# Seven-product steps of passes 6 and 7 of the MLP placed one channel-major step later

## The chip, the core and the metric

The kernel runs on one core of one Trainium2 chip. The metric is the device time of one launch in microseconds (us), median of several runs. A profile is one execution of its own; its times are given from the start of its span.

## What is computed

A trunk of two layers on 256 tokens with 2048 channels, in fp32. Each layer is

```
h = rms_norm(x, norm1_g[l]);  z = h @ w_in[l]            # attention heads and gMLP groups from z
x = x + mix @ w_out[l]                                   # mix: both kinds of groups side by side
h2 = rms_norm(x, norm2_g[l])
x = x + jnp.square(jax.nn.relu(h2 @ w_up[l])) @ w_down[l]   # 2048 -> 8192 -> 2048
```

and a last rms_norm follows. The change lies in the last line, the MLP, of both layers.

## The kernel before, in words

**Products.** Each fp32 factor is split into a high part and a remainder, and a product is three matmuls: high x high, high x remainder of the weight, remainder of the activation x high. Weights come from memory in blocks of 128 x 1024 ("raw", seven buffers), issued by SyncE. ScalarE (ACT) copies a block into its high part ("hi", line 168, six buffers), VectorE (DVE) subtracts that to get the remainder ("lo", line 178, six buffers). So TensorE (PE) needs one hi and one lo for each block.

**Steps.** The program is a list of steps, run in order by the loop at lines 1004 to 1025. Ahead of a step's matmuls the loop issues the hi of blocks up to six on and the lo of blocks up to five on, and whatever small work is due; after them what has to be done with a finished result. A position in time ("soon", "later") is counted in blocks.

A channel-major step (`transposed`, lines 370 to 406) takes one block and makes 24 matmuls of 256 columns: a part of 256 output channels for all tokens. For `w_up` four such steps in a row fill one PSUM bank, for `w_down` two. While the MLP runs, these steps change between banks 0 and 1 (`of=2`). After the last step of a bank of `w_up`, `after_up` (line 779) empties it: ACT makes relu (785), square (788) and the high part of the result (645), DVE its remainder (648); in pass 7 DVE does the relu (787).

A seven-product step (`fast`, lines 408 to 446) multiplies with 512 columns of `w_down` by a scheme of seven products in place of eight. It has two halves, each with two raw blocks, from which DVE makes two more by four subtractions (lines 219 to 224), each gated by ACT's hi. A half takes four lo: top (line 191), bottom, upper and lower (178), in the order in which PE needs them, and counts as four blocks. It makes 42 matmuls; the last three are held back until two matmuls of the next channel-major step have been issued (`BEHIND`, `BETWEEN`).

**Banks of a seven-product step.** Group 0 (output columns 0 to 511) accumulates in held banks ("aux"). Groups 1 and 2 use banks 2 and 3 for four of their products, and borrow, for two more, that one of banks 0 and 1 which the channel-major steps don't use just then (line 863). After the second half, ACT copies the three banks to a staging buffer, the borrowed one first (lines 905 and 906), and later GpSimd's DMAs add the staging buffer to sums in DRAM (`put`, `move`). In a group's last pass (`FINAL`: pass 7 for groups 0 and 1, pass 6 for group 2) the sums are fetched instead, DVE combines them (819 to 827), ACT scales them (832), and PE turns them back by four transposes at line 844, twice.

**Passes.** The loop at line 911 goes through passes e = 0 to 8. Pass e computes hidden channels of eighth e of `w_up` (16 channel-major steps, numbers 0 to 15) and multiplies the eighth before with `w_down`: columns that are not in a group by channel-major steps that follow the up steps (four steps in passes 2 to 6, eight in 1 and 7), and the groups by seven-product steps that stand between. After up step 15, `sums` (line 798) has DVE make four sums of the finished eighth and ACT and DVE split them (645, 648); the seven-product steps of the next pass read them.

**What sets the order.** The table `ORDER` (line 63; passes not named take `USUAL`, line 66) gives for pass e and each group a pair of step numbers: the first half stands right ahead of the first, the second half right ahead of the second. Passes 2 to 5 have group 1 at (2, 3) and group 2 at (13, 14).

Of the kernel before, what the change touches and what calls it, by code (L numbers as in the profile page):

```python
# [59 lines left out]

ORDER = {1: ((7, 10), (13, 14)), 6: ((11, 14), (1, 2), (6, 7)), 7: ((6, 9), (1, 2)), 8: ()}
FINAL = (7, 7, 6)
LAST = (4, 6, 8, 10, 0, 2, 12, 14)
USUAL = ((7, 9), (2, 3), (13, 14))
# [25 lines left out]
def trunk(ctx: ExitStack, tc: tile.TileContext, layout, xT, consts, gains, w, b_sp, w_sp, out):  # L92
# [419 lines left out]
    def layer(l, n1, n2, n3, last):  # L512
# [398 lines left out]
        for e in range(9):  # L911
# [5 lines left out]
            if e:  # L917
                w = 512 * len(ORDER.get(e, USUAL))
                hidden = [hid[e - 1]]
# [3 lines left out]
                               cols=None if e < 8 else [c * P for c in LAST])  # L923
                for g, at in enumerate(ORDER.get(e, USUAL)):
                    banks = []
# [147 lines left out]
```

## Time and profile before

| | |
|---|---|
| Time, median of 3 runs (all) | 2032.55 us (2033.97, 2032.55, 2028.91) |
| The profiled execution | 2032.09 us, span 2030.3 us |
| Busy in the span | PE 99%, weight loads 98%, DVE 78%, ACT 60%, GpSimd 8% |
| Channel-major matmuls, line 404 | 5632 + 2816 on hs, 2688 + 1344 on half, 276 to 277 ns each |
| DVE remainders, line 178 | 817, 1213 ns mean |
| ACT high parts, line 168 | 817, 1051 ns mean |

A matmul lasts some 276 ns, but a new one starts every 0.113 us or so, since they are pipelined; so the share of busy time says little, and the distance between starts says how fast PE runs. In the timelines a row is a start, a duration, the engine, the line, the operation, output<-inputs, their shapes and how many of them were merged; in brackets stands how long the engine was idle ahead of it and what ended that.

### The profile page before, as it was taken

The page shows a single profiled execution, that of the slowest core. Times are in us where ns is not written, and L with a number is a line of the kernel's source. Part 1 is how long each engine was busy: PE and PEld are TensorE (multiplying, and loading weights), DVE is VectorE, ACT ScalarE, POOL GpSimd, SP SyncE. Part 2 cuts the span into 40 slices and gives each one's busy share as a digit, 9 for nine tenths or more (in the row PEclk, how much of TensorE's full clock was granted, in tenths as well). Part 3 has the DMA queues.
Part 4 walks back from the last instruction along what each step waited for, and adds up shares of the span by engine and source line. Part 5 has one row for each costly group of instructions (what it writes and reads, how often), then busy time and mean ns, then how long its engine had stood idle before and what let it go on. Part 6 is the DMA issues. An engine that isn't in the chain of part 4 may idle for free.

```text
span 2030.3 us, 40718 instructions
## 1 busy us (share of the span) xinstructions
PE 2016.9 (99%) x16834; PEld 1979.6 (98%) x16834; DVE 1576.8 (78%) x1950; ACT 1213.2 (60%) x1613; POOL 157.1 (8%) x200
## 2 busy tenths in 40 slices
PE   9999999999999999999999999999999999999997
PEld 7998999999999999999989989999999999999997
DVE  7566766688888898888856667667888898888985
ACT  7565454566566666665545654556666666667654
POOL 0002300000001000100000033000000000010000
PEclk9999999999999999999999999999999999999999
DMA  8554556567677776866664455555676776778562
GB/s 326 192 168 166 187 187 200 175 229 207 217 221 237 244 225 193 243 214 210 204 212 166 167 187 188 188 196 180 217 228 209 226 236 215 239 212 263 183 211 93
DMA packets 126443, 419.27 MB, mean 207 GB/s; under 512 B 14128, under 2 KB 22064, under 8 KB 126256
## 3 DMA queue, kind: packets, MB, share of 16 engines
q1 hardware_dynamic: 110800, 389.86, 56.6%
q0 software_dynamic: 14304, 23.86, 6.8%
q8 instruction: 132, 2.16, 0.4%
q10 hardware_dynamic: 1152, 2.94, 0.4%
q14 instruction: 55, 0.45, 0.1%
HBM read 394.58 MB, written 22.02 MB: 205 GB/s over the span
## 4 chain that ended last, share of the span: by engine, by line
PE 97%; DVE 2%; DMA 1%; ACT 0%; issue 0%; ACTq 0%; SPq 0%; DVEq 0%
PE acc L404 69%; PE acc L434 9%; PE aux L434 8%; PE acc L466 3%; PE acc L465 3%; PE acc L464 3%; DVE lo L178 1%; PE aux L698 0%; PE aux L592 0%; PE aux L634 0%; DMA raw<-in_w 0%; PE aux L621 0%; DVE x L1035 0%; DMA x<-in_xT 0%; PE aux L595 0%
## 5 line engine op out<-in xcount | busy, mean ns | idle before, releaser
L168 ACT ACTIVATE hi<-raw 128x1024 fp32r<-128x1024 f32 (+1 forms) x817 | 836.1, 1051 | 496.2 <-DVE raw L220 232.6
L178 DVE TENSOR_TENSOR lo<-raw,hi 128x1024 fp32r<-128x1024 f32 (+1 forms) x817 | 963.6, 1213 | 155.9 <-ACT hi L168 152.7
L404 PE MATMUL acc<-hs,hi 128*128 128x256 f32 x5632 | 988.1, 277 | 0.0
L404 PEld LDWEIGHTS acc<-hs,hi 128*128 128x128 f32 x5632 | 858.4, 188 | 0.3 <-issue 0.2
L404 PE MATMUL acc<-hs,lo 128*128 128x256 f32 x2816 | 779.0, 277 | 0.0
L404 PEld LDWEIGHTS acc<-hs,lo 128*128 128x128 f32 x2816 | 528.8, 188 | 0.5 <-issue 0.2
L404 PE MATMUL acc<-half,hi 128*128 128x256 f32 x2688 | 462.1, 276 | 0.0
L404 PEld LDWEIGHTS acc<-half,hi 128*128 128x128 f32 x2688 | 406.5, 188 | 0.0
L404 PE MATMUL acc<-half,lo 128*128 128x256 f32 x1344 | 371.1, 276 | 0.0
L404 PEld LDWEIGHTS acc<-half,lo 128*128 128x128 f32 x1344 | 252.4, 188 | 0.0
L871 POOL DMA_DIRECT2D far<-ar x92 | 74.7, 983 | 1158.9 <-ACT ar L874 607.0
L434 PE MATMUL acc<-hi,shared 128*128 128x256 f32 x768 | 139.1, 276 | 0.0
L434 PE MATMUL aux<-hi,half 128*128 128x256 f32 x528 | 120.6, 278 | 0.0
L434 PEld LDWEIGHTS acc<-hi,shared 128*128 128x128 f32 x768 | 119.3, 188 | 0.0
L434 PE MATMUL acc<-lo,shared 128*128 128x256 f32 x384 | 106.5, 277 | 0.6 <-DVE lo L178 0.6
L464 PE MATMUL acc<-hi,hs 128*128 128x512 f32 x256 | 101.3, 396 | 0.2 <-ACT hs L286 0.2
L466 PE MATMUL acc<-hi,hs 128*128 128x512 f32 x256 | 100.8, 394 | 0.0
L465 PE MATMUL acc<-lo,hs 128*128 128x512 f32 x256 | 100.1, 391 | 0.6 <-DVE lo L178 0.6
L648 DVE TENSOR_TENSOR half<-ar,half 128x512 fp32r<-128x512 f32 x72 | 49.7, 690 | 62.3 <-ACT half L645 61.2
L434 PEld LDWEIGHTS aux<-hi,half 128*128 128x128 f32 x528 | 92.9, 188 | 0.0
L434 PE MATMUL aux<-hi,shared 128*128 128x256 f32 x448 | 81.1, 276 | 0.0
L504 DVE TENSOR_TENSOR x<-x,acc 128x512 f32<-128x512 f32 (+1 forms) x49 | 33.0, 674 | 57.7 <-PE acc L404 57.3
(151 smaller groups left out, 1954.0 us busy)
## 6 DMA issues: line engine op xcount, KB each, us to landing
raw<-in_w SPq DMA_DIRECT2D x731, 512.0 KB, 4.6
far<-ar POOLq DMA_DIRECT2D x60, 256.0 KB, 6.3
far<-ar POOLq DMA_DIRECT2D x32, 128.0 KB, 4.4
ar<-far POOLq DMA_DIRECT2D x12, 256.0 KB, 8.9
raw<-in_w SPq DMA_DIRECT2D x10, 256.0 KB, 5.1
x<-in_xT SPq DMA_DIRECT2D x7, 256.0 KB, 5.9
out<-x SPq DMA_DIRECT2D x7, 256.0 KB, 3.0
shared<-in_b_sp ACTq DMA_DIRECT2D x2, 512.0 KB, 8.1
```

The costliest lines, as they stand in the source:

```text
L168: act.activation(self.h[:, j * m:(j + 1) * m], self.raw[:, j * m:(j + 1) * m], AF.Copy)
L178: vec.tensor_tensor(lo[:, r], self.raw[:, r], self.h[:, r].bitcast(F32), op=OP.subtract)
L404: pe.matmul(o, lhsT=lhs, rhs=xs[:, rhs, :], start=(first and j == 0), stop=(last and j == 2), skip_group_check=True)
L434: calls.append(lambda k=k, j=j, lhs=lhs, rhs=rhs: pe.matmul(o[n], lhsT=lhs, rhs=rhs, start=(p == 0 and k == 0 and j == 0 and n in fresh), ...
L464: pe.matmul(ps, lhsT=xh, rhs=hi, start=(k0 + k == 0), stop=False)
L465: pe.matmul(ps, lhsT=xh, rhs=lo, start=False, stop=False)
L466: pe.matmul(ps, lhsT=xl, rhs=hi, start=False, stop=(k0 + k == KC - 1))
L504: vec.tensor_tensor(xj, xj, ps[j][:, 0:S] if alone else pair(ps)[:, j, :], op=OP.add)
L648: vec.tensor_tensor(t[:, c:c + 2, 1, :], src, t[:, c:c + 2, 0, :].bitcast(F32), op=OP.subtract)
L871: nc.gpsimd.dma_start(far[g][:, r], src, **({} if e == max(g, 1) else {"accum_op": OP.add}))
```

## The change

The numbers of passes 6 and 7 in the table each go up by one. Every half of a seven-product step in these passes, with all that is counted from it, comes after one more channel-major step; the last entry, pass 8, has none.

```diff
-ORDER = {1: ((7, 10), (13, 14)), 6: ((11, 14), (1, 2), (6, 7)), 7: ((6, 9), (1, 2)), 8: ()}
+ORDER = {1: ((7, 10), (13, 14)), 6: ((12, 15), (2, 3), (7, 8)), 7: ((7, 10), (2, 3)), 8: ()}
```

The number of instructions stays the same on every engine, and GpSimd's order does not change. Three places show what moves, all in the first layer's pass 6.

VectorE, from the last addition of a `w_down` column of pass 5 (L772) to the lo of "upper" for the second half of group 1; L191 and the four raw rows are that half's. Before:

```order
L772 TENSOR_TENSOR ar_80<-ar_80,acc0_9460 128x512
L178 TENSOR_TENSOR lo_9523<-raw_9312,hi_9489 128x1024
L178 TENSOR_TENSOR lo_9555<-raw_9314,hi_9521 128x1024
L191 TENSOR_TENSOR lo_9603<-raw_9316,hi_9552 128x512
L178 TENSOR_TENSOR lo_9605<-raw_9318,hi_9601 128x1024
L219 TENSOR_TENSOR raw_9316<-raw_9316 128x2x256
L220 TENSOR_TENSOR raw_9316<-raw_9318,raw_9316 128x2x256
L223 TENSOR_TENSOR raw_9318<-raw_9318,raw_9316 128x2x256
L224 TENSOR_TENSOR raw_9318<-raw_9318 128x2x256
L178 TENSOR_TENSOR lo_9617<-raw_9316,hi_9609 128x1024
```

And after the change:

```order
L772 TENSOR_TENSOR ar_80<-ar_80,acc0_9458 128x512
L178 TENSOR_TENSOR lo_9523<-raw_9312,hi_9491 128x1024
L178 TENSOR_TENSOR lo_9555<-raw_9314,hi_9521 128x1024
L178 TENSOR_TENSOR lo_9585<-raw_9316,hi_9552 128x1024
L191 TENSOR_TENSOR lo_9633<-raw_9318,hi_9583 128x512
L178 TENSOR_TENSOR lo_9635<-raw_9352,hi_9631 128x1024
L219 TENSOR_TENSOR raw_9318<-raw_9318 128x2x256
L220 TENSOR_TENSOR raw_9318<-raw_9352,raw_9318 128x2x256
L223 TENSOR_TENSOR raw_9352<-raw_9352,raw_9318 128x2x256
L224 TENSOR_TENSOR raw_9352<-raw_9352 128x2x256
L178 TENSOR_TENSOR lo_9647<-raw_9318,hi_9639 128x1024
```

One lo more, that of the channel-major step that now comes earlier, stands ahead of the half's own.

TensorE, the end of the second half of group 2 and the start of the channel-major step behind it; acc0 and acc1 are banks 0 and 1, and the bank that the half has borrowed is acc1 in both. Before:

```order
L434 MATMUL acc1_9858<-hi_9910,shared_4236 128x256
L434 MATMUL aux_4476<-hi_9910,half_8722 128x256
L434 MATMUL aux_4476<-lo_9918,half_8722 128x256
L434 MATMUL aux_4476<-hi_9910,half_8722 128x256
L404 MATMUL acc0_9794<-hs_85,hi_9912 128x256
L404 MATMUL acc0_9794<-hs_85,lo_9953 128x256
```

And after the change:

```order
L434 MATMUL acc1_9888<-hi_9940,shared_4236 128x256
L434 MATMUL aux_4476<-hi_9940,half_8722 128x256
L434 MATMUL aux_4476<-lo_9948,half_8722 128x256
L434 MATMUL aux_4476<-hi_9940,half_8722 128x256
L404 MATMUL acc1_10055<-hs_85,hi_9942 128x256
L404 MATMUL acc1_10055<-hs_85,lo_9986 128x256
```

Before, the step behind is step 7, which goes on in bank 0; now it is step 8, which opens bank 1, the borrowed one.

ScalarE, from the hi of that half's "upper" to the three copies of the banks. Before:

```order
L168 ACTIVATE hi_9906<-raw_9656 128x1024
L168 ACTIVATE hi_9910<-raw_9716 128x1024
L168 ACTIVATE hi_9912<-raw_9718 128x1024
L168 ACTIVATE hi_9951<-raw_9720 128x1024
L906 ACTIVATE ar_80<-acc1_9858 128x512
L906 ACTIVATE ar_80<-acc2_9856 128x512
L906 ACTIVATE ar_80<-acc3_9857 128x512
```

And after the change:

```order
L168 ACTIVATE hi_9936<-raw_9686 128x1024
L168 ACTIVATE hi_9940<-raw_9746 128x1024
L168 ACTIVATE hi_9942<-raw_9748 128x1024
L785 ACTIVATE ar_80<-acc0_9793 128x512
L788 ACTIVATE ar_80<-ar_80 128x512
L645 ACTIVATE half_9779<-ar_80 128x2x256
L168 ACTIVATE hi_9984<-raw_9750 128x1024
L906 ACTIVATE ar_80<-acc1_9888 128x512
L906 ACTIVATE ar_80<-acc2_9886 128x512
L906 ACTIVATE ar_80<-acc3_9887 128x512
```

The relu, square and high part of up step 7's bank, which stood behind the copies, now stand ahead of them.

## The prediction

> **What bounds the kernel now.** I read the page first, then who waited for whom, then PE's timeline where it waited.
>
> ```profile
> span 2030.3 us, 40718 instructions
> PE 2016.9 (99%) x16834; PEld 1979.6 (98%) x16834; DVE 1576.8 (78%) x1950; ACT 1213.2 (60%) x1613; POOL 157.1 (8%) x200
> PE 97%; DVE 2%; DMA 1%; ACT 0%; issue 0%; ACTq 0%; SPq 0%; DVEq 0%
> PE acc L434 <- DVE lo L178: 0.6, 3, 0.2
> ```
>
> PE is the bound; the change leaves its 16834 matmuls as they are. So only PE's waits and its pace can change. The last line, from the list of waits, names the one kind of wait at line 434, a seven-product half that waits for DVE's lo: three times, 0.6 us. PE's timeline at these places, and at a fourth like them, with the matmul ahead of each wait and the two behind it:
>
> ```profile
> 807.26 0.39 PE L434 MATMUL acc<-hi,shared 128*128 128x256 f32 x2
> 807.85 0.38 PE L434 MATMUL acc<-lo,shared 128*128 128x256 f32 x1 [0.20 <-DVE lo L178]
> 808.08 0.40 PE L434 MATMUL acc<-hi,shared 128*128 128x256 f32 x2
> ...
> 894.18 0.39 PE L434 MATMUL acc<-hi,shared 128*128 128x256 f32 x2
> 894.55 0.39 PE L434 MATMUL acc<-lo,shared 128*128 128x256 f32 x1
> 894.78 0.40 PE L434 MATMUL acc<-hi,shared 128*128 128x256 f32 x2
> ...
> 1812.80 0.39 PE L434 MATMUL acc<-hi,shared 128*128 128x256 f32 x2
> 1813.39 0.39 PE L434 MATMUL acc<-lo,shared 128*128 128x256 f32 x1 [0.20 <-DVE lo L178]
> 1813.62 0.40 PE L434 MATMUL acc<-hi,shared 128*128 128x256 f32 x2
> ...
> 1897.48 0.39 PE L434 MATMUL acc<-hi,shared 128*128 128x256 f32 x2
> 1898.04 0.39 PE L434 MATMUL acc<-lo,shared 128*128 128x256 f32 x1 [0.17 <-DVE lo L178]
> 1898.27 0.28 PE L434 MATMUL acc<-hi,shared 128*128 128x256 f32 x1
> ```
>
> These are the second halves of group 1 in passes 6 and 7 of layer 0, then of layer 1, each at its first use of "upper". A row of two has its second start 0.11 behind the first, so the starts are 0.47, 0.26, 0.48 and 0.45 us apart, and then 0.23, where 0.11 is usual. A wait costs its distance less the usual 0.11, and some 0.12 in the second gap, so about the distance itself: 0.47 + 0.26 + 0.48 + 0.45 = 1.66 us.
>
> They have a consequence that no wait shows. The undisturbed pace is in a row of the chain; the stretches after it are from the table by stretches (its second column is PE's busy time, with the matmuls in brackets; the one ahead of the DMA share is the granted clock).
>
> ```profile
> 612.75 21.55 PE acc L404 x190
> 640.00:680.00 40.00, 40.00 (x355) 40.00 (x354) 35.86 (x40) 28.08 (x35) 4.38 (x5) 1.00 0.78 241
> 812.00:852.00 40.00, 40.00 (x342) 40.00 (x341) 34.84 (x39) 27.29 (x35) 6.62 (x8) 1.00 0.90 263
> 1817.00:1857.00 40.00, 40.00 (x354) 40.00 (x353) 35.41 (x40) 27.86 (x36) 6.99 (x8) 1.00 0.91 268
> 1899.00:1939.00 40.00, 40.00 (x343) 40.00 (x342) 35.00 (x42) 26.80 (x34) 4.08 (x5) 1.00 0.82 263
> 870.02 0.60 PE L844 MATMUL acc<-con,ar 128*128 128x128 f32 x4
> 876.12 0.60 PE L844 MATMUL acc<-con,ar 128*128 128x128 f32 x4
> 1936.19 0.60 PE L844 MATMUL acc<-con,ar 128*128 128x128 f32 x4
> ```
>
> Normally 21.55 / 190 = 0.1134 us a matmul. After the waits at 807 and 1898, 40 us hold 342 or 343 matmuls instead of 355, 3.7% fewer, at a clock of 1.00; after the one at 1813 they hold 354. I call this a tail. It ended at the transposes of 876 (not at those of 870) and of 1936. So two waits of four left long tails: 68.4 us x 0.037 = 2.5 us and 38.3 us x 0.037 = 1.4 us.
>
> All that these four waits cost is 1.66 + 2.5 + 1.4 = 5.6 us of 2032, 0.27%. Two runs of this kernel differ by as much (2028.91 and 2033.97), so 0.3%, some 6.1 us, is about what a measurement can tell from no change.
>
> **Part one: DVE gets time ahead of group 1.** Between the end of pass 5 or 6 and group 1's second half DVE has the sums of the finished eighth and the 4 + 4 subtractions of two halves; it runs without a pause, and PE catches up with it. With the change one channel-major step more, 24 x 0.1134 = 2.72 us of PE, lies in that stretch, and one lo more, some 1.2 us of DVE. The gain is 1.5 us. For pass 6 a direct comparison exists: passes 3 to 5 have group 1 at (2, 3) behind a pass that ended alike. First pass 3's second half on DVE and PE, then pass 6's on DVE, then the stretch of pass 7 in layer 1, first and last row:
>
> ```profile
> 640.98 4.79 DVE L178 TENSOR_TENSOR lo<-raw,hi 128x1024 fp32r<-128x1024 f32 x4
> 643.81 0.28 PE L434 MATMUL acc<-lo,shared 128*128 128x256 f32 x1
> 806.58 4.79 DVE L178 TENSOR_TENSOR lo<-raw,hi 128x1024 fp32r<-128x1024 f32 x4
> ...
> 1875.68 0.69 DVE L648 TENSOR_TENSOR half<-ar,half 128x512 fp32r<-128x512 f32 x1 [2.31 <-ACT half L645]
> 1896.77 4.79 DVE L178 TENSOR_TENSOR lo<-raw,hi 128x1024 fp32r<-128x1024 f32 x4
> ```
>
> A row of four lo lasts 4.79, so the first has ended about 1.2 us after its start: 642.2 in pass 3, where PE takes it at 643.81, 1.6 us in hand; 807.8 in pass 6, where PE takes it at 807.85, nothing in hand. So pass 6 should get what pass 3 has, and both its waits go. In pass 7 the distance from group 0's second half to group 1 stays at seven steps, but the sums, which start at up step 15, get a step more. DVE waited 2.31 us for them at 1875.68, so it has room to start them sooner. By the gain of 1.5, less the 0.34 (0.45 - 0.11) for which PE waited, some 1.2 us are in hand at 1898, and 1.3 at 894. All four waits and both tails go: -5.6 us. If DVE is late for another reason in pass 7, its two waits stay: 0.26 + 0.45 + 1.4 = 2.1 us of it come back.
>
> **Part two: group 2 of pass 6 gives its bank back too late.** Its second half now stands right ahead of step 8, which opens the borrowed bank. PE must wait until ACT has read it. No such wait is in the trace of before, where a step at least lay between; the rows for it are ACT's copies behind this half in both layers, PE's first matmul behind it, and the three operations on an up bank that now come ahead of the copies.
>
> ```profile
> L906 ACT ACTIVATE ar<-acc x72: 593/597/609, 434.6 to 1901.3; 128x512 f32<-128x512 f32 x72
> 834.34 0.28 PE L404 MATMUL acc<-hs,hi 128*128 128x256 f32 x1
> 834.18 1.57 ACT L906 ACTIVATE ar<-acc 128x512 f32<-128x512 f32 x3 [1.88 <-PE acc L434]
> 838.99 0.61 ACT L785 ACTIVATE ar<-acc 128x512 f32<-128x512 f32 x1
> 839.63 0.63 ACT L788 ACTIVATE ar<-ar 128x512 f32<-128x512 f32 x1
> 840.30 0.63 ACT L645 ACTIVATE half<-ar 128x512 fp32r<-128x512 f32 x1
> 1838.91 1.58 ACT L906 ACTIVATE ar<-acc 128x512 f32<-128x512 f32 x3 [1.06 <-PE acc L434]
> ```
>
> The copy of the borrowed bank runs from 834.18 for 0.597, to 834.78; PE would start at 834.34. That is 0.44 us, and 0.05 more from ACT's end to PE's start (as from DVE's 807.80 to PE's 807.85), and 0.11 for the second gap that each wait above shows: 0.60. Then ACT may be late itself: relu, square and high part take 840.93 - 838.99 = 1.94 us, and ahead of the copies ACT had 1.88 us free in layer 0, 1.06 in layer 1. So it would be 0.06 or 0.88 us late. I take 0.07, the value for a half for which DVE is not behind: DVE's subtractions gate the hi's, and with part one it is some 1.5 us further ahead. That is 0.67 us a layer, 1.34 in all, with 1.2 and 3.0 as the ends.
>
> A tail may follow, as behind two waits of four. It would run from step 8 to the second turning back of group 2, now ahead of step 19: eleven steps and group 0's two halves, 11 x 2.72 + 2 x 42 x 0.1134 = 39.5 us, x 0.037 = 1.46 us. I count one of two: 1.46, between 0 and 2.9.
>
> [...]
>
> **Part three: what only moves along.** Group 0's halves, the additions into DRAM, the combining and the transposes keep their distances to their own halves. The additions of group 1 have left the staging buffer long before group 2's copies, since five steps lie between as before. Group 0's last combining ends a step later in pass 8, ahead of steps that end with it only later. Up step 15 now follows right behind group 0's second half in pass 6; DVE's pause of 2.31 us covers that. If it didn't, PE would wait again at pass 7's group 1, the 2.1 us above. I cost this part at nothing.
>
> **The sum.** -5.6 + 1.34 + 1.46 = -2.8 us. The profiled execution took 2032.09 us, 1.8 beside its span and 0.5 below the median of the runs, so 2029.3 us: 0.16% less than the median, which counts as no change.
>
> **The rivals.** First: pass 7's waits stay, because DVE's stretch there is longer than I reckon. For it: nothing is in hand at any of its lo's now. Against: the 2.31 us pause. 2029.3 + 2.1 = 2031.4 us. If ACT is late by 0.88 a layer on top, 2033.0.
>
> Second: new waits leave no tail, because PE waits at the head of a channel-major step and not inside a half; 2029.3 - 1.46 = 2027.8 us. For it: the wait at 1813 left none. [...]
>
> Third, slower: a tail that the transposes do not end. Those of 870 did not. Had it gone on from step 8, near 836 and 1841, to the ends of the layers' MLPs, near 1010 and 2018, it would cost 174 and 177 us x 0.037 = 6.4 and 6.5 us: 2027.8 + 12.9 = 2040.7 us. It decides for slower once the tails of both layers together run for 2.8 / 0.037 = 76 us more than I count. Against: both long tails ended at the second transposes at the latest.
>
> **How the numbers follow.** The forecast has 0.5, the first rival 0.2, the second 0.2, the third 0.05; 0.05 is left for a wait that I don't see. The range goes from 2026.6, a microsecond below the second rival, to 2032.8, the first rival with ACT late. Faster by over 0.3% means below 2026.4. Only the second rival comes near it, and with the spread of the runs of before I give half of it and a little of the forecast: 0.12. Slower by over 0.3%, above 2038.7, is the third rival and a part of the rest: 0.07. No change is the rest, 0.81.
>
> **What would show it.** In the profile after: no wait at line 434 for lo in passes 6 and 7; in pass 6 a wait of half a microsecond in each layer at the first matmul of step 8, with ACT's line 906 as its releaser; starts 0.118 us apart behind one of them, until the transposes. I am wrong if lo waits stay at group 1, if the wait at step 8 is over 1.5 us or missing, or if the pace stays low beyond the transposes.

## The result, and the profile after

| | before | after |
|---|---|---|
| median of 21 runs | 2031.82 us | 2027.72 us |
| fastest and slowest run | 2028.77 to 2033.97 | 2027.17 to 2028.72 |
| profiled execution, span | 2032.09, 2030.3 | 2027.63, 2025.9 |

The ratio on record is 0.9982, with a 95% interval of 0.9977 to 0.9988 (the two medians alone give 0.9980): 0.18% less, clear of the noise, but inside the 0.3% that count as no change. The forecast was 2029.3, the range 2026.6 to 2032.8. Not only the median changed: the runs of after lie within 1.6 us, those of before within 5.2.

From the page after, the span, the busy times and the chain by engine:

```profile
span 2025.9 us, 40700 instructions
PE 2013.1 (99%) x16834; PEld 1976.7 (98%) x16834; DVE 1576.8 (78%) x1950; ACT 1214.9 (60%) x1613; POOL 157.0 (8%) x200
PE 99%; DVE 0%; ACT 0%; issue 0%; DVEq 0%
```

And from the list of PE's waits (the sum in us, how many, the longest) the one line that is about the MLP's middle passes:

```profile
PE acc L404 <- ACT ar L906: 0.7, 2, 0.3
```

The matmuls are the same in number, DVE and ACT work as long as before, and DVE has gone from the chain that ended last. The line for waits on lo at line 434 is gone; a wait on ACT's copy, twice, is new. Group 1's second halves of passes 6 and 7 in layer 0, DVE's four lo with the first use of "upper" on PE:

```profile
807.18 4.79 DVE L178 TENSOR_TENSOR lo<-raw,hi 128x1024 fp32r<-128x1024 f32 x4
810.00 0.28 PE L434 MATMUL acc<-lo,shared 128*128 128x256 f32 x1
...
891.92 4.79 DVE L178 TENSOR_TENSOR lo<-raw,hi 128x1024 fp32r<-128x1024 f32 x4
894.74 0.28 PE L434 MATMUL acc<-lo,shared 128*128 128x256 f32 x1
```

The first lo ends 1.2 us after the row's start, at 808.4 and 893.1: 1.6 us in hand both times (and in layer 1, where they end at 1811.2 and 1895.9, 1.6 again). Then the new wait, in both layers, with the matmul ahead of it and the one behind:

```profile
835.35 0.28 PE L434 MATMUL aux<-hi,half 128*128 128x256 f32 x1
835.98 0.39 PE L404 MATMUL acc<-hs,hi 128*128 128x256 f32 x1 [0.35 <-ACT ar L906]
836.20 0.28 PE L404 MATMUL acc<-hs,lo 128*128 128x256 f32 x1
...
1838.17 0.28 PE L434 MATMUL aux<-hi,half 128*128 128x256 f32 x1
1838.80 0.38 PE L404 MATMUL acc<-hs,hi 128*128 128x256 f32 x1 [0.35 <-ACT ar L906]
```

The starts are 0.63 us apart, then 0.22: a cost of 0.62 us each. And ACT just ahead of its copies in layer 0:

```profile
832.12 0.58 ACT L785 ACTIVATE ar<-acc 128x512 f32<-128x512 f32 x1
832.73 0.64 ACT L788 ACTIVATE ar<-ar 128x512 f32<-128x512 f32 x1
833.40 0.63 ACT L645 ACTIVATE half<-ar 128x512 fp32r<-128x512 f32 x1
833.94 1.05 ACT L168 ACTIVATE hi<-raw 128x1024 fp32r<-128x1024 f32 x1
835.33 1.58 ACT L906 ACTIVATE ar<-acc 128x512 f32<-128x512 f32 x3 [0.34 <-PE acc L434]
```

The relu, square and high part of step 7's bank are there, ahead of the copies, and ACT is still 0.34 us early. The pace of PE, by the table by stretches:

```profile
640.00:680.00 40.00, 40.00 (x355) 40.00 (x354) 35.87 (x40) 27.88 (x35) 4.38 (x5) 1.00 0.81 240
840.00:880.00 40.00, 40.00 (x355) 40.00 (x354) 37.26 (x48) 25.35 (x35) 1.75 (x2) 1.00 0.72 234
1842.00:1882.00 40.00, 40.00 (x355) 40.00 (x354) 37.27 (x48) 26.15 (x36) 1.92 (x3) 1.00 0.75 237
1899.00:1939.00 40.00, 40.00 (x354) 40.00 (x353) 35.93 (x45) 28.19 (x36) 4.09 (x5) 1.00 0.82 264
```

354 or 355 matmuls in 40 us everywhere: there is no long tail, neither the old ones nor one behind the new waits. The span's difference closes with these terms: the four waits of 1.66 us, the tails of 68.4 and 38.3 us at 0.037 (3.9 us), less 2 x 0.62, are 4.3 us; the spans differ by 4.4.

### The profile page after: what moved, and what is told of

Read it like the earlier page. It is cut to its first block, busy times and chain, and to the rows that moved or that the text cites. A ratio compares the mean times of both kernels' runs of the same rounds, so it can differ in the third digit from the quotient of the medians.

```text
span 2025.9 us, 40700 instructions
## 1 busy us (share of the span) xinstructions
PE 2013.1 (99%) x16834; PEld 1976.7 (98%) x16834; DVE 1576.8 (78%) x1950; ACT 1214.9 (60%) x1613; POOL 157.0 (8%) x200
## 4 chain that ended last, share of the span: by engine, by line
PE 99%; DVE 0%; ACT 0%; issue 0%; DVEq 0%
PE acc L404 70%; PE acc L434 10%; PE aux L434 8%; PE acc L466 3%; PE acc L464 3%; PE acc L465 3%; PE aux L698 0%; PE aux L592 0%; PE aux L634 0%; PE aux L621 0%; PE aux L991 0%; DVE x L1035 0%; PE aux L595 0%; PE aux L636 0%; PE acc L844 0%; PE aux L533 0%
```

## The experiments

My theory: DVE's time ahead of group 1 is what the change buys; group 2's bank costs 0.6 us a layer; a tail is a state that PE falls into at a wait. Against it: the gain comes from where group 2 stands; or the waits go only to come back a group later; or the tails come from the work beside PE. All ten kernels were timed in rounds with the kernel before on the same chip; the ratio is to that. The rounds were on three chips, where the kernel before had medians of 2030.73 us (group 1 only, group 2 only, all but group 2, the copies), 2030.99 (pass 6, pass 7, small matmuls, borrowed bank first) and 2032.27 (the repeats on DVE), against 2031.82 beside the changed kernel. So medians of different rounds compare only to a microsecond or two, and the changed kernel itself was not in these rounds.

**Only group 1 moved.**

```diff
-6: ((11, 14), (1, 2), (6, 7)), 7: ((6, 9), (1, 2))      # before
+6: ((11, 14), (2, 3), (6, 7)), 7: ((6, 9), (2, 3))
```

> Only group 1 is moved in passes 6 and 7, to (2, 3); groups 0 and 2 stay as before. Theory: the whole gain is group 1's lo waits and the tails behind them, and group 2 of pass 6 has a step between its second half and the step that opens the borrowed bank, so there is no bank wait either. That is the time of the changed kernel (2027.7) less its two waits of 0.6: 2026.5 us, 0.26% under before, with runs within some 1.5 us of each other, no lo wait at group 1 and no wait on ACT's line 906. Rival: with three steps in place of four between group 1 and the next group DVE falls behind there, and the lo waits and tails come back one group later: 2029 to 2032 us with the spread of 5 us of before.

Measured: 2033.68 us (2032.5 to 2035.57), ratio 1.0009 (1.0000 to 1.0018). My number failed, and the rival has the mechanism, though the time lies above its range too. The lo waits went from group 1 and came back in the halves of the next group and behind it. The largest, in pass 7 behind group 0's second half, in both layers, from the list of waits:

```profile
PE acc L404 <- DVE lo L178: 2.7, 2, 1.3
```

In the timeline of layer 0, PE there, and DVE's work that fills the time ahead of it:

```profile
924.07 0.28 PE L404 MATMUL acc<-hs,hi 128*128 128x256 f32 x1
925.68 0.39 PE L404 MATMUL acc<-hs,lo 128*128 128x256 f32 x1 [1.33 <-DVE lo L178]
...
921.57 0.42 DVE L819 TENSOR_TENSOR ar<-ar 128x256 f32<-128x256 f32 x1
...
924.07 0.42 DVE L827 TENSOR_TENSOR ar<-ar 128x256 f32<-128x256 f32 x1
924.41 2.35 DVE L178 TENSOR_TENSOR lo<-raw,hi 128x1024 fp32r<-128x1024 f32 x2
```

Starts 1.61 us apart. DVE combines group 1's sums there (lines 819 to 827, 921.57 to 924.49), and the lo comes after it. With three steps in place of four between two groups DVE has 1.5 us less to catch up, and the wait that was saved ahead of group 1 is paid behind it. Behind both of these waits PE also kept the slow pace for 8.8 us, up to the next transposes. So the step ahead of group 1 alone is worth nothing: the others have to move with it.

**The change without group 2's part.**

```diff
-6: ((12, 15), (2, 3), (7, 8))      # after
+6: ((12, 15), (2, 3), (6, 7))
```

> The changed kernel with group 2 of pass 6 put back to (6, 7); groups 0 and 1 as changed. Theory: the bank wait goes, all else stays: 2027.7 - 1.2 = 2026.5 us, the same as with group 1 alone moved, and no wait on line 906. Rival, that three steps between group 1 and group 2 are too few for DVE: lo waits at group 2's halves of some 0.3 us each and their tails, 2028 to 2030 us.

Measured: 2028.38 us (2028.0 to 2031.44), ratio 0.9987 (0.9979 to 0.9996). The bank wait went, and a lo wait in group 2's second half came for it, in both layers alike:

```profile
829.91 0.39 PE L434 MATMUL acc<-hi,shared 128*128 128x256 f32 x2
830.57 0.38 PE L434 MATMUL acc<-lo,shared 128*128 128x256 f32 x1 [0.26 <-DVE lo L178]
```

0.54 us between starts: the rival's mechanism, at a price close to the bank wait's. Of its eleven runs nine are within 1.7 us and two near 2031.3, as long tails would leave them; no profile caught one, so that is not shown.

**Only group 2 moved.**

```diff
-6: ((11, 14), (1, 2), (6, 7))      # before
+6: ((11, 14), (1, 2), (7, 8))
```

> Only group 2 of pass 6 is moved, from (6, 7) to (7, 8). Theory: the four lo waits at group 1 and their tails stay, and a wait of 0.62 us on ACT's copy of the borrowed bank comes in each layer: 2031.8 + 1.2 = 2033.0 us at the median, unless the new wait also ends a tail that runs then (each us of tail cut short gives 0.037 us; layer 0's would lose 40 of 68 us, 1.5 us). Rival, that the gain of the change came from where group 2 stands and group 1's waits were only where PE met it: under 2030 us.

Measured: 2033.2 us (2030.7 to 2034.04), ratio 1.0006 (0.9997 to 1.0015). As the theory has it: 0.62 between starts at step 8 in both layers, group 1's waits still there in pass 6, and by the ratio some 1.2 us more than before, though its interval includes none. One wait I had not foreseen came in pass 7 of both layers, with starts 0.58 us apart, for DVE's line 504, and group 1's lo waits behind it are gone; the next kernel shows the same.

**Only pass 6 moved, only pass 7 moved.**

```diff
-6: ((11, 14), (1, 2), (6, 7)), 7: ((6, 9), (1, 2))      # before
+6: ((12, 15), (2, 3), (7, 8)), 7: ((6, 9), (1, 2))      # pass 6 alone
+6: ((11, 14), (1, 2), (6, 7)), 7: ((7, 10), (2, 3))     # pass 7 alone
```

> Only pass 6 is changed, pass 7 stays at (6, 9), (1, 2). Theory: pass 6's two lo waits and their tails go and its two bank waits of 0.62 come; in pass 7 group 1's first half comes one step too early for the bank that group 2's second turning back uses, a wait of 0.58 for DVE's line 504 in each layer as with group 2 alone moved, which gives DVE the time that its lo's lacked there. That is the changed kernel's 2027.7 plus two waits of 0.6 and, behind them, tails now and then: 2029 to 2030.5 us. Rival, that pass 7 needs no shift of its own: 2027.7 us.

> Only pass 7 is changed, pass 6 stays at (11, 14), (1, 2), (6, 7). Theory: pass 7's two lo waits (0.26 and 0.45 us) and the tails behind them go; pass 6's stay (0.47 and 0.48 us and now and then a tail of up to 2.5 us): 0.7 to 2.1 us under before, 2029 to 2030.5 us, and runs that differ by up to 5 us still. Rival, that a step more between the passes makes DVE fall behind elsewhere: no gain, 2031 us.

Pass 6 alone: 2031.23 us (2029.61 to 2033.37), ratio 1.0000 (0.9992 to 1.0009). That is above the 2029 to 2030.5 expected. The predicted wait is there, and in layer 1 it left a tail of some 47 us. PE at the wait in layer 0:

```profile
883.66 0.28 PE L434 MATMUL acc<-hi,half 128*128 128x256 f32 x1
884.28 0.35 PE L434 MATMUL acc<-hi,shared 128*128 128x256 f32 x1 [0.35 <-DVE x L504]
```

And by the table by stretches the pace behind it, in layer 0 and then in layer 1:

```profile
888.00:928.00 40.00, 40.00 (x352) 39.85 (x351) 37.15 (x46) 28.27 (x36) 3.56 (x4) 1.00 0.75 229
1892.00:1932.00 40.00, 40.00 (x342) 40.00 (x342) 36.91 (x45) 27.69 (x35) 3.50 (x4) 1.00 0.74 225
```

Group 2's second turning back uses bank 3, DVE adds it to x, and pass 7's group 1 wants the bank. So pass 7 has to move too when pass 6 does.

Pass 7 alone: 2028.44 us (2027.31 to 2031.35), ratio 0.9990 (0.9982 to 0.9999). That is under the 2029 to 2030.5 expected. In its profile only pass 6's two lo waits are left (0.49 between starts). Its runs fall into two groups, six at 2027.3 to 2028.4 and five at 2029.6 to 2031.4. They differ by about 2.3 us, which is what one long tail in pass 6 costs (60 to 68 us x 0.037). The profile, with no long tail, is of the first group; no run of the second was profiled. The first group is as fast as the changed kernel: the two waits that stay cost 2 x 0.49 us, the changed kernel's bank waits 2 x 0.62. What moving pass 6 as well seems to add is the absence of the second group: none of the 21 runs of the changed kernel is above 2028.8.

**More work for DVE in group 1's second halves,** on the changed kernel: the lo of top made again, two or four times, the same values into the same place.

```diff
+            if p and col0 == 512 and row0 >= 5 * 1024 and not (row0 == 7 * 1024):
+                top.again = 2                      # 4 in the other
...
-            vec.tensor_tensor(self.lo, self.left(), self.hi.bitcast(F32), op=OP.subtract)
+            for _ in range(1 + self.again):
+                vec.tensor_tensor(self.lo, self.left(), self.hi.bitcast(F32), op=OP.subtract)
```

> The changed kernel, but DVE makes the lo of top twice more than needed (the same values into the same place, 0.60 us each) in the second half of group 1 in passes 6 and 7. Theory: with the change DVE has 1.61 us in hand at the upper lo of all four halves (1.56 at the next step's), so 1.2 us of useless work there is swallowed: no lo wait, 0.4 us in hand, the time of the changed kernel, 2027.7 us. Rival, that those waits went because something else than DVE's time was set right: a DVE delay shows at once, 4 x 1.2 us = 4.8 us, or the time is the same also with twice as much.

> As before, with four repeats of the lo of top in place of two, 2.4 us of DVE in each of the four halves. Theory: 0.8 us more than DVE has in hand: four lo waits return, each a gap of some 0.95 us between starts (0.84 over the usual) and 0.12 behind it, 3.8 us, and behind some of them a long tail (up to 2.5 us in layer 0 and 1.4 to 2.3 us in the others): 2031.5 us without a long tail, 2031.5 to 2036 us in all, with runs that differ by several us again. Rival: no lo wait, 2027.7 us.

Measured: 2029.83 us (2027.97 to 2031.1), ratio 0.9988 (0.9979 to 0.9997) with two; 2036.26 us (2034.15 to 2038.32), ratio 1.0021 (1.0012 to 1.0030) with four, just above the 2036 given as the most. With four, from the list of waits:

```profile
PE acc L437 <- DVE lo L178: 4.1, 4, 1.0
```

And in PE's timeline at pass 6's group 1:

```profile
809.98 0.57 PE L437 MATMUL acc<-hi,shared 128*128 128x256 f32 x2
811.57 0.38 PE L437 MATMUL acc<-lo,shared 128*128 128x256 f32 x1 [1.02 <-DVE lo L178]
```

All four waits are back. A repeat costs 0.72 us, not 0.60 (the next view has three in 2.14); 4 x 0.72 - 1.6 = 1.3 us, and the starts are 1.41 apart, 1.3 over the usual. That is the theory's account of the 1.6 us in hand, to a tenth. With two repeats 0.15 us is left, there is no wait worth the name, and yet the time rose: the median is 2.1 us above the changed kernel's, by the ratios 1.2 us with intervals that overlap, and the profile's span is 1.2 us longer, 2027.1. DVE's three subtractions, and PE where it had waited:

```profile
802.72 2.14 DVE L192 TENSOR_TENSOR lo<-raw,hi 128x512 fp32r<-128x512 f32 x3
810.05 0.30 PE L437 MATMUL acc<-lo,shared 128*128 128x256 f32 x1
810.19 0.40 PE L437 MATMUL acc<-hi,shared 128*128 128x256 f32 x2
```

The pace behind that place and later, from the table by stretches:

```profile
812.00:836.00 24.00, 24.00 (x206) 24.00 (x206) 21.72 (x25) 17.52 (x23) 3.52 (x4) 1.00 0.89 269
840.00:880.00 40.00, 40.00 (x354) 40.00 (x353) 37.27 (x49) 26.36 (x36) 2.13 (x3) 1.00 0.75 235
```

The two starts are 0.14 apart instead of 0.11, 0.02 to 0.03 us. Behind that hitch 24 us hold 206 matmuls (8.6 a us) where 40 hold 354 later (8.85): a tail, up to the bank wait at step 8, which ended it. So a wait need hardly be one to start a tail, and the four waits of before were worth more than they lasted.

**What a tail is.** The kernel before, with four small matmuls that add zeros at the end of up step 2 in passes 6 and 7.

```diff
+                if name == "w_up" and col0 >= 6 * 1024 and c == 0 and k0 == 8:
+                    for _ in range(4):
+                        pe.matmul(o[0:64, 0:P], lhsT=tri[64:P, 0:64], rhs=ident[64:P, :], start=False, stop=False,
+                                  skip_group_check=True)
```

> The kernel before, with four small fp32 matmuls that add zeros (64 rows, 64 x 128) at the end of up step 2 in passes 6 and 7 of both layers, 2.7 us behind the lo waits; nothing else. Theory: a long tail is a state of PE's own pace that a few matmuls of another shape end, as the transposes do; then no tail is longer than some 5 us, the runs lie within 2 us of each other in place of 5, and the median is that of the fastest runs of before, 2028.8, plus what the 16 small matmuls cost (four transposes take 0.35 us: 1.4 us), 2030.2 us. Rival, that a tail comes from what DVE, ACT and the DMAs do beside PE: the tails stay, 2031 + 1.4 = 2032.4 us with a spread of 5 us.

Measured: 2039.07 us (2037.17 to 2040.68), ratio 1.0043 (1.0030 to 1.0055). Both numbers failed. The small matmuls are dearer than transposes (1.0 us for four, against 0.35), and they start tails. The extra matmuls in pass 6 of layer 0:

```profile
813.24 1.08 PE L408 MATMUL acc<-con 64*64 64x128 f32 x8
814.25 0.38 PE L404 MATMUL acc<-hs,hi 128*128 128x256 f32 x1
```

And a stretch behind those of layer 0 and one behind those of layer 1:

```profile
816.00:856.00 40.00, 40.00 (x342) 40.00 (x341) 34.32 (x40) 26.05 (x34) 4.44 (x5) 1.00 0.87 260
1826.00:1866.00 40.00, 40.00 (x342) 40.00 (x341) 34.21 (x39) 26.96 (x35) 4.38 (x5) 1.00 0.83 253
```

The slow pace begins at the matmul behind them at three of the four places and lasts until the turning back's transposes, 62.7, 38.7 and 62.7 us; the lo waits ahead of these three left short tails, which were over by then. At the fourth, pass 7 of layer 1, the tail of the lo wait was still running. A row of two and the single matmul after it make three:

```profile
1909.26 0.40 PE L404 MATMUL acc<-hs,hi 128*128 128x256 f32 x2
1909.61 0.40 PE L404 MATMUL acc<-hs,hi 128*128 128x256 f32 x2
...
1910.17 1.08 PE L408 MATMUL acc<-con 64*64 64x128 f32 x8
...
1912.22 0.39 PE L404 MATMUL acc<-hs,hi 128*128 128x256 f32 x2
1912.56 0.39 PE L404 MATMUL acc<-hs,hi 128*128 128x256 f32 x2
```

Three matmuls take 0.35 us ahead of the small ones and 0.34 behind them: here they ended a tail. So the theory that a few matmuls of another shape end one held at the only place that could test it; what it missed is that they begin one where none runs. The three tails that began speak against the rival: the work beside PE is that of before, and what began them is a break in PE's own stream. What it is inside PE, and why the same matmuls end it at one place and begin it at three, the runs don't tell.

**The borrowed bank.** On the changed kernel, first only the order of ACT's copies, the borrowed bank last; then the order of the banks, so that the borrowed one is filled first, and copied first again.

```diff
-                for i in (2, 0, 1):                # both
+                for i in (0, 1, 2):
...
-            banks[:] = [acc_bank(2), acc_bank(3), acc_bank(1 - bank_at[0])]      # second kernel only
+            banks[:] = [acc_bank(1 - bank_at[0]), acc_bank(2), acc_bank(3)]
```

> The changed kernel, but ACT copies the borrowed bank last of the three instead of first, everywhere. Theory: the copies start 0.49 us apart, so PE's wait at step 8 grows from 0.62 to 1.6 us start to start in both layers: 2027.7 + 2.0 = 2029.7 us if the longer waits leave no long tail, up to 2032.6 if both do (1.46 each). Where a step lies between (group 1, passes 1 to 5) the copies are done in time and nothing changes. Rival, that the wait is not ACT's copy but the staging buffer or a DMA: no change, 2027.7 us.

> The changed kernel, but groups 1 and 2 put their first two products into the borrowed bank instead of the last two, and ACT copies it first as before. Theory: the wait at step 8 is only that ACT reads the borrowed bank after the last of its products; with those products 30 matmuls (3.4 us) ahead of the half's end the copy (0.6 us) is long done, no wait is left on line 906, and the time is 2027.7 - 1.2 = 2026.5 us. Rival, that PE then waits at the first half instead, where the borrowed bank must be empty 2.7 us sooner (DVE's line 772 empties it in passes 6 and 7): 0.3 to 1 us of new waits a place, 2027 to 2029 us.

With the borrowed bank copied last: 2028.22 us (2027.76 to 2029.16), ratio 0.9982 (0.9973 to 0.9991), no different from the changed kernel. My number failed, though not for the rival's reason: the wait is still ACT's copy, and 0.62 long.

```profile
834.47 1.62 ACT L906 ACTIVATE ar<-acc 128x512 f32<-128x512 f32 x3
836.14 0.38 PE L404 MATMUL acc<-hs,hi 128*128 128x256 f32 x1 [0.35 <-ACT ar L906]
```

The copies of banks 2 and 3 now run while the half still multiplies, since those banks are finished first; the third copy then waits for PE as it did before. What fixes the wait here is the bank that PE finishes last, not the order of copying. With the borrowed bank filled first and copied first: 2026.85 us (2026.45 to 2027.13), ratio 0.9981 (0.9972 to 0.9990). ACT's copies and PE at the place of the wait:

```profile
834.47 1.63 ACT L906 ACTIVATE ar<-acc 128x512 f32<-128x512 f32 x3
835.53 0.28 PE L434 MATMUL aux<-hi,half 128*128 128x256 f32 x1
835.65 0.28 PE L404 MATMUL acc<-hs,hi 128*128 128x256 f32 x1
```

No wait is left at lines 404 and 434, and the slowest of its runs is as fast as the fastest of the changed kernel. By the medians it is 0.9 us under it, where 1.2 was expected, but those are of different rounds, and the two ratios are alike. The traces decide: from a layer's first seven-product matmul to its last channel-major one, PE takes 612.1 us here and 612.7 in the changed kernel, in both layers, 0.6 less in each as expected. No other version measured has times as low.

## Why the prediction was right, and where it was not

**The bound and the size of the prize.** Right: PE's waits and its pace are all that moved, and the 5.6 us that I gave as the most there was to win set the verdict. The profiles' difference is those 5.6 us less the new waits. A fifth wait of before, 0.2 us at line 404 near 925.9, I had left out; it is gone too.

**Part one.** Right in mechanism and nearly in size: the 1.6 us in hand taken over from pass 3 were 1.6 in pass 6, and 1.6 in pass 7 too, where I had worked out 1.2 and 1.3. The four repeats on DVE show that it is DVE's time. The first rival, pass 7's waits staying, did not happen.

**Part two.** The wait is there, at the place and with the releaser that I named, in both layers; 0.60 a layer was reckoned and 0.62 measured. My 0.07 for a late ACT was not needed: DVE being further ahead made its gate open sooner (in layer 0 the hi's that wait for DVE's last subtraction began 5.1 us ahead of the copies, 4.8 before), and ACT was 0.34 us early.

**The tail behind it** is the step that failed, a term of the sum that was sized too large: "I count one of two: 1.46". There was none in the profile, and the spread of 1.6 us over 21 runs leaves little room for one. This was the second rival, with 0.2, whose 2027.8 us is what was measured. That it fits to 0.1 us has luck in it: the sum starts from one execution with two long tails, in a kernel whose runs spread over 5.2 us, and that one lay 0.3 us from the median of the 21. The rival's reason, that a wait at the head of a channel-major step is unlike one inside a half, is borne out by count, not by a cause: in the six profiles that have the bank wait (two each) PE is back at its pace within a microsecond all twelve times (354 or 355 matmuls in the 40 us from 840 in the changed kernel, with pass 6 alone and with two repeats on DVE), and in two of them, with the DVE repeats, the bank wait even ended a tail that ran into it (206 matmuls in 24 us ahead of it and 354 in 40 behind it with two, 215 in 25 and 223 in 25 with four). But with group 1 alone moved, the two waits of 1.5 us stand only one matmul further on, at the second of a step, and each left 8.8 us of slow pace. So where exactly a wait stands matters; that it is the head of a step which matters is not shown. Nor does the granted clock tell a tail from the usual pace: it was 1.00 in the stretches with 342 matmuls in 40 us, in before, with pass 6 alone and with the small matmuls, as in those with 354.

**Part three.** "I cost this part at nothing" gave the right sum, but it was too light a way to put it. Moving the other groups along is what the gain rests on: group 1 alone moved gave nothing back, pass 6 alone neither, and pass 7 alone, with both its groups, a part (ratio 0.9990). The reason that I gave, equal distances, is the right one; I had not seen how little is in hand behind group 1, where a step less brings waits of up to 1.5 us.

**The numbers.** 2029.3 was 1.6 us above the measured median: 1.46 of it is the tail.

## What to carry to other kernels

DVE and PE run close together at several places here, and a step inserted ahead of one place moved the shortage to the next (waits of up to 1.5 us, ratio 1.0009); what gained was to move the whole group so that the distances between the places stay (0.9982). A buffer that is given back and taken again at once should be the first that is finished, not the first that is copied: with the borrowed bank copied first or last the wait was 0.62 us, with the bank filled first there was none. And look at the distance between starts behind a wait, not only at the wait: here 3.9 of the 5.6 us that four waits cost lay in the slower pace after them.

## What the runs showed of the hardware

After a break in its stream PE went on at times at 117 to 118 ns a matmul instead of 113.4, at a granted clock of 1.00, for 3 us or for as long as 68 (in before behind the waits of 1813 and of 807). With two repeats on DVE a hitch of 0.02 to 0.03 us was enough to start it. Of 33 stretches of slow pace that began inside a seven-product half, counted in the traces in passes 6 and 7, 23 were short and ended with the half, where its last three matmuls alternate with the first two of the next step (in before at 1816.7, 3.3 us behind the wait of 1813). The other ten went past that place and, unless a new wait came, past every later one like it, as behind the wait of 807 in before. These long tails ended at a set of four transposes (in before those of 876 and of 1936, though not those of 870), at a bank wait (with the DVE repeats), or at eight matmul instructions of 64 x 128 in fp32 (three matmuls in 0.35 us ahead of them, in 0.34 behind). The same eight began one at the three places where none was running (62.7, 38.7 and 62.7 us).

Whether a tail got long differed from profile to profile: the wait of pass 6 in layer 0 left 68 us in before and some 3 us in the profiles with group 2 alone, pass 7 alone and the small matmuls, where PE's matmuls are the same up to there. That this makes most of the spread of the kernel before (5.2 us) is likely, as the two groups of runs with pass 7 alone suggest, but no two runs of one kernel were profiled. What decides it stays open.
